# The last output projection: eight gated tiles multiplied by two weight blocks at a time in seven quarter products

## The chip, the cores and the metric

The kernel runs on one core of a Trainium2 chip. The metric is the device time of one execution, in microseconds (us). The time before is 1355.15 us, the median of three runs (1355.09 to 1355.34). TensorE (PE) multiplies matrices, VectorE (DVE), ScalarE (ACT) and GpSimd (POOL) work elementwise, and SyncE (SP) starts most transfers.

## The reference, cut to what matters

A two-layer trunk over 512 prompt tokens and 32 sample tokens. Layer 0 is an RWKV mixer, layer 1 a differential attention with twelve heads and a memory attention with four. Each layer ends in a gated branch of width 2048 and an output projection to width 1024:

```python
def diff_layer(...):
    ...
    o = rmsnorm(o, subln) * (1.0 - lam_init)
    y_mem = mem_attention(qm, mk, mv)
    out = jnp.concatenate([o.reshape(B, T, MIX_W).astype(x.dtype), y_mem], axis=-1) * jax.nn.silu(gate)
    return x + out @ w_out, k, v
...
y_prompt = rmsnorm(xp, final_norm_w)
y_sample = rmsnorm(xs, final_norm_w)
```

The change is about `out @ w_out` of layer 1, which is a 544x2048 by 2048x1024 product, and about what follows it, `x +` and the last `rmsnorm`.

## The kernel before, in words

Everything is kept transposed: features lie on the 128 partitions, tokens along the row. T = 544 tokens are cut in two halves of TH = 272. The gated branch is sixteen tiles `og0` to `og15` of 128x544 (`self.o1`). Tiles 0 to 7 are heads that are finished early; tiles 8 to 11 are the last four attention heads, and 12 to 15 the memory heads. The residual and the result is `x1` (128 x 8 x 544).

A product in fp32 is made from three matmuls. Each factor is split in a rounded high part and the rest: `hi = round(x)` is a copy on ACT, `lo = x - hi` is a subtraction on another engine, and hi·hi, lo·hi and hi·lo are accumulated in PSUM. A weight block is a column block of 128 outputs by 1024 inputs, loaded as two pieces of 256 KB (128x4x128); `split` makes `whi` and `wlo` from it, in two instructions each (128x512).

The output projection of layer 1 is `w_out`: eight output blocks k, sixteen tiles, two token halves and three matmuls, 768 matmuls of 128x272. It adds each finished block to `x1` in `consume`, which also squares it (ACT, `sqn`) and adds the squares up (DVE, `sums`). `consume` also issues the transposes of the finished `x1` to token rows (`ps_f`, on PE), the totals of the squares (`ps_n`, on PE), the last normalisation (`og<-ps_f`) and the stores of the result. After each finished pair of halves it starts one transfer of keys and values to the output (`kv_out`).

Ahead of it stands the main stream of layer 1 (`diff_layer`). A list of events `at(step, function)` puts attention work between the matmuls of the input projection, and while `self.ordered` is set every engine keeps the order of the program. The last head has seven blocks of 48 matmuls, 336 steps, counted from f. In it the split of gated tiles 4 to 7 is made at the steps `LATE` = 186, 222, 254 and 290. After the stream the remaining events run: the four heads of the last group are normalised (`norms`, the `oss` and `nt` operations), scaled (`ot<-ot,oss`), transposed by PE (`ps_oT`) and gated (`finished`, `og<-ps_oT`).

After the main stream the order is not the program's any more. A scheduler places the instructions by its own estimate of times, except on a queue that `self.tied` names, which is SP alone before. So the `ps_oT`, `ps_f` and `ps_n` work of PE lies where the scheduler finds place between the matmuls of `w_out`. A third pair of weight buffers (`self.third`, `w3`) serves every third block.

The helper through which nearly all instructions are recorded is one line, L132 before and L133 after, so operations are told apart by the names of their tiles.

Of the kernel before, what the change touches and what calls it, by code (L numbers as in the profile page):

```python
# [18 lines left out]
P = 128  # L19
# [46 lines left out]
NGATED = 8  # L66
EARLY = 4
# [67 lines left out]
class Trunk:  # L135
# [273 lines left out]
    def split(self, raw):  # L409
# [3 lines left out]
        third = self.third is not None and self.turn % 3 == 2  # L413
        self.turn += 1
        if third:
            both = self.third.tile([P, 2, KT, P], F32R, tag="hl", name="w3")
            hi, lo = both[:, 0], both[:, 1]
        else:
            hi, lo = (self.wp.tile([P, KT, P], F32R, tag=x, name=x, bufs=2) for x in ("whi", "wlo"))
# [910 lines left out]
    def gated(self, g, hi, lo, t):  # L1330

        self.ae.copy(hi[:], t)
        (self.nc.gpsimd if g % 2 and not self.third else self.ve).tensor_tensor(lo[:], t, hi[:].bitcast(F32), ALU.subtract)
# [14 lines left out]
    def w_out_blocks(self, i):  # L1348

        w = self.a["w_out"][i]  # L1350
        todo = [(0, 0), (1, 0), (0, 1), (1, 1)] + [(k, q) for k in range(2, KT) for q in range(2)]
        return [(w[q * D : (q + 1) * D, :], k * P) for k, q in todo]

    def w_out(self, i, p, order, consume, extra=None, o=None):
# [26 lines left out]
        if i:  # L1381
            units += units[-2:]
            parts[-2:] = [[halves[:1]]] * 2 + [[halves[1:]]] * 2

        def products():
            for n, ((k, q, gs, last), part) in enumerate(zip(units, parts)):
# [8 lines left out]
                for vs in part:  # L1395
                    for j, g in enumerate(gs):
                        if k < 2 and (j + k) % 2 == 0 and n >= first:
                            ahead(1)
                        if i and n == 1 and j == 2:
                            self.used()  # L1400
# [15 lines left out]
        return products(), ahead  # L1416

# [394 lines left out]
    def layer1(self):  # L1812
# [3 lines left out]
        self.o1 = [op.tile([P, T], F32, name=f"og{g}") for g in range(16)]  # L1816
        with ExitStack() as ectx:
            made, order = {}, list(range(8)) + [12, 13, 14, 15, 8, 9, 10, 11]
            with ExitStack() as c2:
# [5 lines left out]
                self.kz = [dq.tile([P, 2, T], F32R, name=f"kz{i}") for i in range(2)]  # L1825
# [4 lines left out]
                kv_out = self.diff_layer(dq, p, mp, mctx, lambda: self.pool("wo1e", 1, ctx=ectx, side="right"), order, made)  # L1830
# [3 lines left out]
            self.third, self.turn, self.tied = self.h0, 2, self.se  # L1834
# [32 lines left out]
            def consume(k, ps, v):  # L1867
# [3 lines left out]
                if k >= 2 and kv_out:  # L1871
                    kv_out.pop(0)()
# [12 lines left out]
            for _ in self.w_out(1, po, order, consume, o=made)[0]:  # L1885
                pass
        self.hctx.close()

    def stream(self, makes):

        def nxt():
            if self.made:
                return self.made.pop(0), []
            return self.split(self.early.pop(0))
# [22 lines left out]
        for fn, _ in cur[1]:  # L1917
            fn()
# [517 lines left out]
```

## Time and profile before

| what | value |
|---|---|
| median of three runs | 1355.15 us |
| the profiled execution | 1360.9 us |
| its span, first to last instruction | 1359.1 us |
| PE busy | 1304.9 us, 96% |
| DVE busy | 922.2 us, 68% |
| ACT busy | 856.3 us, 63% |
| POOL busy | 630.8 us, 46% |
| mean granted TensorE clock | 0.989 |

The profiled execution is 5.75 us longer than the median of the timed runs; 1.8 us of it lie outside its span. Positions below are us from the start of that span. The main stream of layer 1 ends at 1245.0, the matmuls of the output projection run from there to 1348.4, and the span ends at 1359.1. In a view of the timeline a row gives the start, the length, the engine, the line, the operation, its output and inputs, the shapes and the count; in square brackets stands how long the engine had waited and for what. Rows that follow each other closely on one engine overlap by a pipeline's depth, so the step from one to the next is a little shorter than the length.

### The profile page before, as it was taken

The numbers are of one execution on the slowest core, as the hardware profiler recorded it, in microseconds if no ns is written. First come the engines' busy times: TensorE is split into PE (matmuls) and PEld (weight loads), VectorE is DVE, ScalarE is ACT, GpSimd is POOL, SyncE is SP. The second block draws the span as 40 slices with busy tenths as digits, with TensorE's granted clock in tenths as the row PEclk, the third lists the DMA queues.
The fourth block names the chain that finished last, engine by engine and source line by source line (L and its number), as shares of the span: only waits on it lengthen the run. The fifth ranks groups of instructions, "written<-read, shape, count | busy, mean of one in ns | idle before, by whom it ended". The sixth has DMA issues, their size and how long they took to land. (4 is left out here: it accounts for less than half of the span.)

```text
span 1359.1 us, 32016 instructions
## 1 busy us (share of the span) xinstructions
PE 1304.9 (96%) x11713; PEld 1192.7 (88%) x11713; DVE 922.2 (68%) x2391; ACT 856.3 (63%) x2316; POOL 630.8 (46%) x1103
## 2 busy tenths in 40 slices
PE   6999999999999999989999999999999999999997
PEld 6998899999999999888889998888887887788997
DVE  6766667877787768766574453656697666877543
ACT  6665677677767777665554346777676776774421
POOL 1317675567556755660021007756555665662000
PEclk9999999999999999999999999999999999999999
DMA  7643223322332232232356444767677768774461
GB/s 235 183 118 78 61 69 87 78 73 73 87 78 70 76 87 74 55 104 73 114 186 202 130 133 130 172 160 177 148 185 164 174 156 183 172 172 115 143 203 66
DMA packets 418295, 171.52 MB, mean 126 GB/s; under 512 B 195209, under 2 KB 402578, under 8 KB 418138
## 3 DMA queue, kind: packets, MB, share of 16 engines
q1 hardware_dynamic: 417994, 168.96, 48.0%
q8 instruction: 92, 1.51, 0.5%
q14 instruction: 65, 0.53, 0.1%
q10 hardware_dynamic: 144, 0.52, 0.1%
HBM read 130.84 MB, written 41.92 MB: 127 GB/s over the span
## 5 line engine op out<-in xcount | busy, mean ns | idle before, releaser
L132 PE MATMUL ps_g<-h,whs 128*128 128x272 f16 x2688 | 334.1, 281 | 3.6 <-POOL whs L132 3.6
L132 PEld LDWEIGHTS <-whs 128*128 128x128 f16 x2688 | 256.9, 98 | 57.7 <-POOL whs L132 5.3
L132 PE MATMUL ps_g<-hl,whi 128*128 128x272 f32 x960 | 281.5, 298 | 0.6 <-POOL hl L591 0.5
L132 PE MATMUL ps_g<-hh,wlo 128*128 128x272 f32 x912 | 277.9, 305 | 1.3 <-DVE wlo L132 1.3
L132 PE MATMUL ps_g<-hh,whi 128*128 128x272 f32 x912 | 275.1, 302 | 0.9 <-ACT hh L132 0.9
L880 POOL TENSOR_TENSOR tm<-u,m 102x84 f32<-102x84 f32 (+23 forms) x372 | 157.3, 423 | 165.4 <-DMA m<-sc 134.8
L132 DVE TENSOR_TENSOR wlo<-raw,whi 128x512 fp32r<-128x512 f32 x194 | 140.8, 739 | 64.6 <-ACT whi L132 63.4
L132 PEld LDWEIGHTS ps_g<-hl,whi 128*128 128x128 f32 x960 | 181.6, 191 | 2.4 <-POOL hl L591 0.7
L132 PEld LDWEIGHTS ps_g<-hh,whi 128*128 128x128 f32 x912 | 174.8, 192 | 4.4 <-ACT hh L132 1.3
L132 PEld LDWEIGHTS ps_g<-hh,wlo 128*128 128x128 f32 x912 | 174.3, 191 | 4.8 <-DVE wlo L132 2.1
L882 POOL TENSOR_TENSOR u<-u,tm 102x84 f32<-102x84 f32 (+23 forms) x372 | 160.4, 431 | 29.1
L132 POOL TENSOR_TENSOR whs<-h16s,whs 128x512 f16<-128x512 f32 x112 | 130.7, 1187 | 51.4 <-ACT whs L132 49.7
L132 ACT CAST whi<-raw 128x512 fp32r<-128x512 f32 x194 | 116.2, 616 | 58.1 <-PE ps_g L132 31.0
L132 POOL TENSOR_SCALAR h16s<-h16s 128x512 f32<-128x512 f32 x112 | 79.1, 719 | 89.0 <-DVE h16s L132 83.0
L132 PE MATMUL ps_g<-hi,whi 128*128 128x272 f32 x384 | 110.7, 288 | 0.9 <-ACT whi L132 0.9
L132 PE MATMUL ps_g<-lo,whi 128*128 128x272 f32 x384 | 110.7, 288 | 0.7 <-DVE lo L132 0.7
L132 PE MATMUL ps_g<-hi,wlo 128*128 128x272 f32 x384 | 110.6, 288 | 0.2 <-DVE wlo L132 0.2
L132 DVE SCALAR_TENSOR_TENSOR SB<-ps_c,dl,sd 64x64 f32<-64x64 f32 x168 | 47.4, 282 | 43.5 <-PE ps_c L132 39.1
L132 PEld LDWEIGHTS ps_g<-hi,whi 128*128 128x128 f32 x384 | 72.2, 188 | 1.2 <-ACT whi L132 1.2
L132 PEld LDWEIGHTS ps_g<-lo,whi 128*128 128x128 f32 x384 | 72.2, 188 | 1.1 <-DVE lo L132 1.1
L132 PEld LDWEIGHTS ps_g<-hi,wlo 128*128 128x128 f32 x384 | 72.3, 188 | 0.4 <-DVE wlo L132 0.4
L132 ACT CAST whs<-h16s 128x512 f16<-128x512 f32 x112 | 65.4, 619 | 9.5 <-POOL h16s L132 7.7
(437 smaller groups left out, 2935.0 us busy)
## 6 DMA issues: line engine op xcount, KB each, us to landing
raw<-in_rw_in_dram SPq DMA_DIRECT2D x114, 256.0 KB
h16s<-in_df_in_dram SPq DMA_DIRECT2D x112, 256.0 KB
raw<-in_w_out_dram SPq DMA_DIRECT2D x56, 256.0 KB
ptr<-pk SPq DMA_DIRECT2D x44, 160.0 KB
aT<-ptr SPq DMA_DIRECT2D x11, 640.0 KB
scr<-sg SPq DMA_DIRECT2D x96, 68.0 KB
out_dram<-scr SPq DMA_DIRECT2D x6, 1024.0 KB
m<-sc SPq DMA_DIRECT2D x36, 128.0 KB
```

Of the source, the lines that this page charges most:

```text
L132: return lambda *a, **k: self.trunk.tie(self, issue(*a, **k))
L880: nc.gpsimd.tensor_tensor(tm[:, :n, :wd], u3[:, :n, kx : kx + 1].to_broadcast(sh), m3[:, kx : kx + 1, kx + 1 :].to_broadcast(sh), ALU.mult)
L882: nc.gpsimd.tensor_tensor(u3[:, :n, kx + 1 :], u3[:, :n, kx + 1 :], tm[:, :n, :wd], ALU.add)
```

## The change

The product of tiles 0 to 7 with the eight output blocks is made by Strassen's method in Winograd's form. For a pair of output blocks (n = 0 to 3) the weight is cut in four quarters (input half by output block), the tiles in four (four tiles by token half, 128 x 4 x 272). Seven products of a quarter sum with a quarter sum replace eight. Each is a group of 4 x 3 = 12 matmuls; 28 groups make 336 matmuls where 384 were. Tiles 8 to 15 are multiplied as before (384 matmuls).

Around that:

- **Weights.** For each pair four sums of weight pieces on DVE (`sum`, 128x512), seven copies on ACT, six subtractions on POOL and one on DVE (`ws`). Group t prepares group t + 3. The sums lie in the same four raw buffers (`h16s`) through which the pieces are loaded; the order of the pieces is now all first input halves, then all second ones.
- **Tokens.** Seven quarter sets in high and low parts, each in two instructions of 128x544: sets 1, 2 and 3 are raw quarters (steps 40 and 100 of heads 10 and 11, 186 and 222 of the last), with the low part on POOL; sets 7, 6, 4 and 5 are differences (`d7`, `d6`, `d4`, `d5` on DVE), made and split at the steps 258 to 343 of the last head.
- **Results.** Each product is added to, or subtracted from, `x1` by DVE (`add`, 128x272), eight times for a pair.
- **Order.** After the stream PE is tied to the program's order as SP is (`self.tied` is now a pair). The remaining events run between the matmuls of the groups, and `finished` moves from b + 30 to b + 48. The `kv_out` transfers start one for every 24 matmuls.
- **Removed.** The third weight buffer; the subtraction for odd gated tiles is on POOL again.

```diff
-        if self.ordered or self.tied is queue:
+        if self.ordered or self.tied and queue in self.tied:
...
-        third = self.third is not None and self.turn % 3 == 2
...
-        (self.nc.gpsimd if g % 2 and not self.third else self.ve).tensor_tensor(lo[:], t, hi[:].bitcast(F32), ALU.subtract)
+        (self.nc.gpsimd if g % 2 else self.ve).tensor_tensor(lo[:], t, hi[:].bitcast(F32), ALU.subtract)
...
+        if i:
+            todo = [(k, q) for q in range(2) for k in range(KT)]
...
+    def parted(self, to, x, q, low):
+        hi, lo = to[0][q], to[1][q]
+        self.ae.copy(hi, x)
+        low.tensor_tensor(lo, x, hi.bitcast(F32), ALU.subtract)
+    def seven(self, blocks, sets, groups, add, free):
...
+        def prepare(t):
...
+            if i == 7:
+                sum_of(n, 3, a11, a21)
+            if i == 6:
+                sum_of(n, 1, a21, a22)
+                sum_of(n, 2, sums[n, 1], a11)
+            if i == 4:
+                sum_of(n, 4, sums[n, 2], a12)
...
+            self.ae.copy(hi, x)
+            def low():
+                (self.ve if i == 5 else self.ge).tensor_tensor(lo, x, hi.bitcast(F32), ALU.subtract)
...
+        def products():
...
+                for k in range(4):
+                    for j, (w, x) in enumerate(((hi, xh), (hi, xl), (lo, xh))):
+                        if k == 0 and j == 0:
+                            low = prepare(t + 3)
+                        if k == 1 and j == 1:
+                            low()
...
+    def w_out1(self, blocks, load, sets, tiles, add, consume):
+        groups = [(2, 0), (1, 0), (2, 1), (7, 0), (6, 0), (1, 1), (4, 0), (5, 0), (7, 1), (3, 0), (6, 1), (4, 1), (2, 2), (5, 1)]
+        groups += [(1, 2), (7, 2), (3, 1), (6, 2), (4, 2), (2, 3), (5, 2), (1, 3), (7, 3), (3, 2), (6, 3), (4, 3), (5, 3), (3, 3)]
...
+            for n, (k, vs) in enumerate([(k, halves) for k in range(KT - 2)] + [(k, [v]) for v in halves for k in (KT - 2, KT - 1)]):
...
+            def add(k, v, ps, up):
+                x = self.x1[:, k, v]
+                self.ve.tensor_tensor(x, x, ps, ALU.add if up else ALU.subtract)
...
-            self.third, self.turn, self.tied = self.h0, 2, self.se
...
-                        at(b + 30 + 14 * j, lambda G=G, hg=hg, j=j: finished(G, hg, j))
+                        at(b + 48 + 14 * j, lambda G=G, hg=hg, j=j: finished(G, hg, j))
...
+                plan = [(186, lambda: raw_set(3, 0)), (222, lambda: raw_set(3, 1)), (258, lambda: fresh(7))]
+                plan += [(258 + 8 * q, lambda q=q: differ(7, q, B[0, 1][q], B[1, 1][q])) for q in range(2)]
+                plan += [(286, lambda: (fresh(6), fresh(4)))]
+                plan += [(286 + 4 * q, lambda q=q: differ(6, q, tmp[7][q], B[0, 0][q])) for q in range(2)]
+                plan += [(294 + 4 * q, lambda q=q: differ(4, q, tmp[6][q], B[1, 0][q], ALU.add)) for q in range(2)]
+                plan += [(300 + 6 * q, lambda q=q: split(7, q)) for q in range(2)]
+                plan += [(312 + 6 * q, lambda q=q: split(6, q)) for q in range(2)]
+                plan += [(290 + 16 * t, lambda t=t: begun(t)) for t in range(3)]
+                plan += [(337, late)] + [(337 + q, lambda q=q: split(4, q)) for q in range(2)]
+                plan += [(338, lambda: fresh(5))] + [(339 + q, lambda q=q: differ(5, q, B[0, 0][q], B[0, 1][q])) for q in range(2)]
+                plan += [(341 + q, lambda q=q: split(5, q)) for q in range(2)]
...
-        self.used()
-        self.ordered = False
+        self.ordered, self.tied = False, (self.te, self.se)
         while ev:
-            ev.pop(0)[2]()
+            i += 1
+            while ev and ev[0][0] <= i:
+                ev.pop(0)[2]()
+            next(begun(None))
```

Three places show how instructions stand now. The first is DVE in the last head, from one attention output to the weights of the next scores (`ot` is the output of the third of the last four heads, `pt` the scores' weights for PE's transposes). Before:

```order
L132 TENSOR_SCALAR h16s<-dv,h16s 128x1
L132 TENSOR_TENSOR ot<-ps_o,os_16820 128x512
L132 TENSOR_TENSOR kz_12354<-og_12335,kz_12354 128x544
L132 TENSOR_REDUCE oss<-ps_o 128x4
L132 SCALAR_TENSOR_TENSOR og_12339<-og_12339,ps_g 128x272
L132 COPY os<-ps_os 128x128
L132 RECIPROCAL srs<-srs 128x1
```

The same place of the changed kernel:

```order
L133 TENSOR_SCALAR h16s<-dv,h16s 128x1
L133 TENSOR_TENSOR sum<-h16s 128x512 x2
L133 TENSOR_TENSOR sum<-sum,h16s 128x512 x2
L133 TENSOR_TENSOR sum<-h16s 128x512
L133 TENSOR_TENSOR ot<-ps_o,os_16805 128x512
L133 TENSOR_TENSOR d_18262<-og 128x544
L133 TENSOR_REDUCE oss<-ps_o 128x4
L133 SCALAR_TENSOR_TENSOR og<-og,ps_g 128x272
L133 COPY os<-ps_os 128x128
L133 TENSOR_TENSOR d_18262<-og 128x544
L133 RECIPROCAL srs<-srs 128x1
```

Five weight sums stand ahead of `ot`, the last of them of weight pieces that are loaded late, and the two halves of `d7` stand where the split of tile 6 (`kz`) was.

The second place is DVE after the stream, from the last head's square totals (`oss`) to its scaled output (`ot<-ot,oss`), for which PE's transposes `ps_oT` wait. Before, the middle of it:

```order
L132 SCALAR_TENSOR_TENSOR oss<-nt_18473,oss 128x16
L132 TENSOR_TENSOR w_18582<-h16s,w_18582 128x512
L132 TENSOR_TENSOR nt_18473<-oss 128x16
L132 TENSOR_TENSOR w_18582<-h16s,w_18582 128x512
L132 TENSOR_TENSOR nt_18473<-nt_18473,oss 128x16
L132 SCALAR_TENSOR_TENSOR nt_18473<-nt_18473 128x16
L132 SCALAR_TENSOR_TENSOR oss<-nt_18473,oss 128x16
L132 TENSOR_TENSOR ot<-ot,oss 128x512 x3
```

The same of the changed kernel:

```order
L133 TENSOR_TENSOR x_10643<-x_10643,ps_g 128x272
L133 SCALAR_TENSOR_TENSOR oss<-nt_18473,oss 128x16
L133 TENSOR_TENSOR late<-d_18484,late 128x544
L133 TENSOR_TENSOR nt_18473<-oss 128x16
L133 TENSOR_TENSOR x_10643<-x_10643,ps_d 128x272
L133 TENSOR_TENSOR nt_18473<-nt_18473,oss 128x16
L133 SCALAR_TENSOR_TENSOR og<-osT,h16s,og 128x32
L133 SCALAR_TENSOR_TENSOR nt_18473<-nt_18473 128x16
L133 SCALAR_TENSOR_TENSOR og<-osT,h16s,og 128x32
L133 SCALAR_TENSOR_TENSOR oss<-nt_18473,oss 128x16
L133 TENSOR_TENSOR sum<-sum,h16s 128x512
L133 TENSOR_TENSOR ot<-ot,oss 128x512 x4
```

The chain is now interleaved with the additions to `x1` (which wait for PE), with two low parts (`late`) and with a weight sum. PE's first `ps_oT` stands, in its fixed order, behind 50 matmuls of the groups.

The third place is the end of PE's order, at the second to last block of the first token half and the one behind it. Before:

```order
L132 MATMUL ps_g<-lo_17527,w_19340 128x272
L132 MATMUL ps_f<-ident,x_10643 128x128 x2
L132 MATMUL ps_g<-hi_17526,w_19340 128x272
L132 MATMUL ps_g<-hi_17727,w_19340 128x272
L132 MATMUL ps_g<-lo_17728,w_19340 128x272
L132 MATMUL ps_g<-hi_17727,w_19340 128x272
L132 MATMUL ps_g<-hi_17872,w_19340 128x272
L132 MATMUL ps_n<-ones,sums 128x1 x2
L132 MATMUL ps_g<-lo_17873,w_19340 128x272
```

The same of the changed kernel:

```order
L133 MATMUL ps_g<-lo_18690,whi 128x272
L133 MATMUL ps_g<-hi_18689,wlo 128x272
L133 MATMUL ps_n<-ones,sums 128x1 x2
L133 MATMUL ps_f<-ident,x_10643 128x128 x2
L133 MATMUL ps_g<-hi_18675,whi 128x272
L133 MATMUL ps_g<-lo_18676,whi 128x272
```

The totals `ps_n` stood ten matmuls behind the block whose squares they add up, and stand now directly behind its last matmul; the other transposes `ps_f` are placed in the same way.

More of the change, by code (lines that the diff above doesn't have):

```diff
@@ L66 @@
 NGATED = 8
+RAW_SETS = {1: (0, 0), 2: (1, 0), 3: (1, 1)}
 EARLY = 4
@@ L412, in split @@
             return self.split_scaled(raw)
-        third = self.third is not None and self.turn % 3 == 2
[L414 to L419, printed above, removed]
+        hi, lo = (self.wp.tile([P, KT, P], F32R, tag=x, name=x, bufs=2) for x in ("whi", "wlo"))
         todo = []
@@ L1815, in layer1, with load, begun @@
         op = self.pool("o1", 1)
-        self.o1 = [op.tile([P, T], F32, name=f"og{g}") for g in range(16)]
+        self.og = op.tile([P, 16, T], F32, name="og")
+        self.o1 = [self.og[:, g] for g in range(16)]
         with ExitStack() as ectx:
-            made, order = {}, list(range(8)) + [12, 13, 14, 15, 8, 9, 10, 11]
+            sets, tiles, steps, blocks = {}, {}, [], []
+            def load():
+                if self.ahead:
+                    for _ in self.load_steps(*self.ahead.pop(0)):
+                        pass
+                    blocks.append(self.early[-1])
+            def begun(t):
+                if not steps:
+                    blocks.extend(self.early)
+                    while len(blocks) < 4:
+                        load()
+                    steps.extend(self.w_out1(blocks, load, sets, tiles, add, lambda *x: steps[2](*x)))
+                return steps[1] if t is None else steps[0](t)()
+            def add(k, v, ps, up):
+                x = self.x1[:, k, v]
+                self.ve.tensor_tensor(x, x, ps, ALU.add if up else ALU.subtract)
             with ExitStack() as c2:
@@ L1883, in consume, with gate @@
                     last((2, 3, 4) if v.start else (0, 1))
-            for _ in self.w_out(1, po, order, consume, o=made)[0]:
-                pass
+            steps.append(consume)
+            left = [12, 13, 14, 15, 8, 9, 10, 11]
+            tiles.update((g, self.fetch(po, g)) for g in left)
+            def gate(g):
+                tiles[g] = self.gated(g, *tiles[g])
+            for n, _ in enumerate(steps[1]):
+                if n % 24 == 23:
+                    if left:
+                        gate(left.pop(0))
+                    if kv_out:
+                        kv_out.pop(0)()
         self.hctx.close()
@@ L2396, in run @@
         self.early, self.made, self.ahead = [], [], []
-        self.third, self.turn, self.inner, self.rec, self.tied = None, 0, False, None, None
+        self.inner, self.rec, self.tied = False, None, None
         self.mctx = ExitStack()
```

136 lines of the change are left out of this document (110 added, 26 removed).

## The prediction

> **What bounds the kernel now.** First the busy shares and the granted clock on the page, then the windows of the output projection, then the chain of work that ended last.
>
> ```profile
> PE 1304.9 (96%) x11713; PEld 1192.7 (88%) x11713; DVE 922.2 (68%) x2391; ACT 856.3 (63%) x2316; POOL 630.8 (46%) x1103
> ...
> 1225.00:1235.00 10.00, 10.00 (x93) 8.15 (x91) 5.77 (x17) 5.17 (x14) 4.44 (x5) 1.00 0.78 214
> 1235.00:1245.00 10.00, 9.92 (x88) 8.66 (x86) 7.73 (x22) 4.87 (x12) 3.81 (x3) 1.00 0.26 73
> 1245.00:1252.00 7.00, 6.67 (x55) 6.48 (x53) 6.38 (x22) 3.22 (x7) 0.00 (x0) 1.00 0.00 0
> 1260.00:1300.00 40.00, 40.00 (x323) 39.85 (x323) 20.38 (x38) 13.09 (x27) 0.00 (x0) 1.00 0.55 173
> 1300.00:1340.00 40.00, 40.00 (x323) 39.87 (x322) 12.64 (x24) 8.10 (x16) 0.00 (x0) 1.00 0.38 122
> ...
> 1300.31 30.62 PE ps_g L132 x245
> ```
>
> In a row of the windows stand the stretch, its length, and busy us (and count) of PE, PE's weight loads, DVE, ACT and POOL, then the granted clock, 1.00 here. PE never rests from 1225 on but for 0.4 us, and POOL does nothing at all in the projection. In the chain 245 matmuls in a row take 30.62 us, 0.125 us each. So a matmul less is 0.125 us less, as long as PE stays as busy; and a wait of PE, which is nearly nothing now, is a loss in full:
>
> ```profile
> PE ps_n L132 <- DVE sums L132: 0.5, 1, 0.5
> PE ps_oT L132 <- DVE ot L132: 0.3, 1, 0.3
> PE ps_f L132 <- DVE x L132: 0.2, 1, 0.2
> ```
>
> These are all of PE's waits from 1225 to the end (us, times, longest).
>
> **What the change removes.** 384 matmuls become 336: 48 x 0.125 = **6.0 us less** on PE. The weight loads are as many as the matmuls and fit beside them now (39.85 of 40 us). This is certain; the rest is what new waits take back. I go through PE's fixed order at three places.
>
> **The last head.** DVE's rows, with those of SP and PE, from the timeline and the chain of before (the short rows are the chain's):
>
> ```profile
> 1229.74 0.69 DVE L132 TENSOR_TENSOR ot<-ps_o,os 128x512 f32<-128x512 f32 x1 [1.62 <-PE ps_o L132]
> ...
> 1238.09 0.44 DVE L132 SCALAR_TENSOR_TENSOR og<-og,ps_g 128x272 f32<-128x272 f32 x1 [1.68 <-ACT og L132]
> ...
> 1239.07 0.75 DVE L132 SCALAR_TENSOR_TENSOR pt<-ps_s,srs,pt 128x512 f32<-128x512 f32 x1
> ...
> 1228.31 2.63 SPq L132 DMA_DIRECT2D h16s<-in_w_out_dram  x2
> ...
> 1202.08 2.01 DMA scr<-sg
> ...
> 1230.53 0.60 ACT ps_o L132
> 1231.13 0.30 ACT pk L132
> ...
> 1231.71 0.43 PE L132 MATMUL ps_os<-cv,aTs 128*32 128x128 f32 x8
> ...
> 1239.97 0.63 PE L132 MATMUL ps_aT<-ident,pt 128*128 128x128 f32 x4
> ```
>
> Five weight sums now stand ahead of `ot`. The idle 1.62 us before it hold two and a half of them (0.64 each, from `wlo`, 1.28 for two, below). The fifth needs the seventh weight piece, which SP issues at 1228.31, when POOL has freed its buffer; I take 2.0 us for the transfer, the length of `scr<-sg`, the nearest one in the chain of waits. The piece is there near 1230.4, and `ot` follows at 1231.1 instead of 1229.74, 1.4 us late. PE's `ps_os` waits behind `ot` and two short ACT steps of the chain, which ended at 1231.43, so 0.3 us of that are covered: 1.1 us of PE at least. With the sums held up by POOL (next paragraph) I find up to 3.7. Ahead of `pt` stand three more pieces of 128x544, the second half of `d6` and both of `d4`, behind an `og` that now ends the idle time: 3 x 0.66 = 2.0 us, less the 0.15 between `pt`'s end (1239.82) and `ps_aT`. So 1.8 us without contention, and up to 5 with. The start of the projection moves by **3 to 9 us; I take 5**, nearer the rows without contention, since POOL's idle times leave room.
>
> **The engines' contention.** What two engines do to each other is in these rows:
>
> ```profile
> 1238.67 1.34 POOL L1333 TENSOR_TENSOR vhl<-og,khl 128x544 fp32r<-128x544 f32 x1 [8.12 <-ACT khl L132]
> 1239.98 2.50 POOL L132 TENSOR_TENSOR wlo<-h16s,whi 128x512 fp32r<-128x512 f32 x2
> ...
> 1240.17 1.10 DVE L132 SCALAR_TENSOR_TENSOR nt<-os 128x1 f32<-128x1 f32 x1
> 1241.30 1.19 DVE L132 TENSOR_TENSOR nt<-nt,os 128x1 f32<-128x1 f32 x1
> 1242.53 0.16 DVE L132 SCALAR_TENSOR_TENSOR os<-nt,os 128x1 f32<-128x1 f32 x1
> ```
>
> One DVE operation on a single column takes 1.10 us while POOL's first `wlo` runs, the next 1.19 while the second runs, and 0.16 as soon as POOL is done: DVE stood still for the whole of POOL's operation. The projection is free of this before, with POOL at 0.00; the change puts 26 POOL subtractions there (22 `ws`, four `lo` of odd tiles).
>
> [...]
>
> **The groups.** DVE's list between the last `ot` and the scaled `ot`, for which `ps_oT` waits:
>
> ```profile
> 1246.47 1.28 DVE L132 TENSOR_TENSOR wlo<-h16s,whi 128x512 fp32r<-128x512 f32 x2
> ...
> 1248.74 0.68 DVE L132 TENSOR_TENSOR w<-h16s,w 128x512 fp32r<-128x512 f32 x1
> 1249.34 0.17 DVE L132 TENSOR_TENSOR nt<-oss 128x16 f32<-128x16 f32 x1
> 1249.43 0.68 DVE L132 TENSOR_TENSOR w<-h16s,w 128x512 fp32r<-128x512 f32 x1
> ...
> 1250.65 1.90 DVE L132 TENSOR_TENSOR ot<-ot,oss 128x512 f32<-128x512 f32 x3
> ...
> 1251.48 0.63 PE L132 MATMUL ps_oT<-ident,ot 128*128 128x128 f32 x4 [0.33 <-DVE ot L132]
> ...
> L132 DVE TENSOR_TENSOR x<-ps_g,x 128x272 f32<-128x272 f32 x16 | 6.9, 442 | 25.0 <-PE ps_g L132 25.0
> ...
> L132 DVE TENSOR_TENSOR lo<-og,hi 128x544 fp32r<-128x544 f32 x8 | 5.3, 719 | 0.0
> L132 ACT CAST whi<-raw 128x512 fp32r<-128x512 f32 x16 | 9.1, 619 | 22.3 <-PE ps_g L132 17.3 <-issue 4.2 <-ACT sums L132 0.8
> ```
>
> Four low parts go (2.5 us by their steps). In come two `d5` and two `late` at 0.66 (5.3 us for eight, in the groups by line), three additions to `x1` at 0.44 and a sum at 0.64: 4.6 us, of which 0.6 fit in an idle piece ahead of `oss`. `ot` is ready 1.5 us later against PE, which comes 2 to 3 matmuls (0.3 us) later, and already waited 0.33. PE is tied, so nothing moves up into the gap: **1.5 us**. POOL has there two `late` of 1.34 (by `vhl`) and three `ws` of 1.25 (by its `wlo`), 6.4 us, against DVE operations that read two tiles; if DVE stands still for all of it the wait is 7.9 us. Behind that, POOL has 21 operations of about 1.25 us (26 us) and DVE some 20 two-operand ones holding about 0.5 us (10 us), 36 us in 35 us of matmuls for the remaining groups: 0 to 4 us more. **1.5 to 12 us; I take 5**, as POOL must run in that stretch but DVE's additions read PSUM and need not stop.
>
> The eight additions for a pair (32 x 0.44 = 14 us) and the casts of ACT (28 x 0.62 = 17 us, by `whi<-raw`, 619 ns) stand beside 42 us of matmuls, on engines that were busy for half of the time and a third: nothing. If that cover were gone each group would wait 0.44 for its addition, 12 us; groups on the same bank are two or more groups apart, so I leave it at nothing. The `kv_out` transfers go on SP, now between weight pieces; the DMA share there is 0.55 at most, also nothing.
>
> **The end.** PE is tied behind each wait for `x1` or for `sums`:
>
> ```profile
> 1295.59 0.87 PE ps_f L132 x8
> ...
> 1296.07 0.69 DVE L132 TENSOR_TENSOR og<-ps_f,fw 128x512 f32<-128x512 f32 x1
> ...
> 1296.81 0.66 PE L132 MATMUL ps_f<-ident,x 128*128 128x128 f32 x4
> ...
> 1330.97 0.44 DVE L132 TENSOR_TENSOR x<-ps_g,x 128x272 f32<-128x272 f32 x1 [1.20 <-PE ps_g L132]
> 1331.97 0.44 DVE L132 TENSOR_TENSOR sums<-sums,sqn 128x272 f32<-128x272 f32 x1 [0.56 <-ACT sqn L132]
> ```
>
> From a block's last matmul to the end of `x` are 0.55 us, to the end of `sums` (1332.41) 1.45. Twenty `ps_f` in a row wait 0.55, then have two banks, which DVE empties in 0.7 us each with one `sums` between, for five: 4.0 us in all where the transposes alone need 2.2 (eight in 0.87 in the chain, which is the first row): 1.8. Six, then six again: 0.55 each. `ps_n`: 1.45. Sum 4.35, less the 0.2 that is there now: **4.1 us** (2.5 if the banks don't bind and a neighbouring wait covers one of them, 5 at most). The last `ps_n`, behind the last block, is the same in both kernels.
>
> **The sum.** Against the profiled execution's 1360.9 us (span 1359.1): -6.0 + 5 + 5 + 4.1 = +8.1. The timed median is 5.75 us lower for the same program, and I carry the difference over: 1355.15 + 8.1 = **1363 us**.
>
> **The rivals.**
> - *As above*, three waits of moderate size: 1363, from 1358 to 1370. Chance 0.45.
> - *The lock decides.* Every POOL operation stops a two-operand one of DVE, so the upper ends hold: -6 + 9 + 12 + 4.1 = +19, **1374 us**. For it speaks the doubled `nt` above; against it, that many DVE operations read PSUM. [...] Chance 0.2.
> - *Only the end stays.* DVE's additions in the last head fit in its idle times and `ps_oT` is not late, because POOL is ahead: -6 + 4.1 = -1.9, **1353 us**, within 0.2%. Against it speaks the fifth sum's load, for which DVE stands still. Chance 0.15.
> - *The saving arrives: faster.* One mechanism, in the last head: the weight pieces land before 1229, since their buffers come free earlier, so that all sums fit in DVE's 1.62 idle us and everything on DVE and POOL stays ahead of PE to the end of the groups. Then the end at its lower price is what is left: -6 + 2.5 = -3.5, **1351.6 us**. It decides at the seventh piece: 1.5 us earlier or not. Chance 0.2.
>
> That the matmuls are not fewer can be left out: the order of PE shows 336.
>
> **The range.** 0.2% (2.7 us) is about what a measurement of this kernel tells from no change. Faster by more: the last case, 0.2. Within: the third, 0.15. Slower: 0.65. From 1350.5, which takes in the faster case but for its edge, to 1376, with the lock's case: about 0.8 with what lies beyond either. The forecast's own range is 1358 to 1370.
>
> **What would show it.** Right: in the waits of PE from 1225 on, `ps_os` or `ps_aT` behind DVE's `ot` or `pt` with 1 us or more each; `ps_oT` behind `ot` with 1.5 or more; `ps_n` behind `sums` with two waits near 1.4; `ps_f` behind `x` and `og`. The stage's POOL busy goes from 0 to about 30 us, and DVE's `sum` and `late` are longer than 0.7 in the mean. Wrong: the projection's start still at 1245; PE at 40 of 40 in each window; or two-operand operations of DVE at 0.66 beside POOL.

## The result and the profile after

The changed kernel takes 1377.47 us, the median of six runs (1374.28 to 1382.05); the kernel before took 1355.14 us beside it (six runs, 1353.15 to 1355.8). The ratio, here and below taken over the single runs and not from the two medians, is 1.0169, with a 95% interval from 1.0149 to 1.019: slower, by about 22 us. The sign is the forecast's. The size is not: 1363 was forecast, and the time lies 7.5 us beyond the forecast's own range (1358 to 1370) and 1.5 us beyond the wide one (up to 1376), nearest to the rival in which the lock decides (1374).

The profiled execution took 1382.05 us (span 1380.3). Its busy line and all of PE's waits from 1200 us on (total us, times, longest):

```profile
PE 1310.2 (95%) x11665; PEld 1194.4 (87%) x11665; DVE 957.6 (69%) x2433; ACT 870.0 (63%) x2334; POOL 679.8 (49%) x1135
...
PE ps_g L133 <- DVE x L133: 5.2, 2, 2.9
PE ps_aT L133 <- DVE pt L133: 4.2, 2, 3.3
PE ps_g L133 <- DVE oss L133: 3.8, 1, 3.8
PE ps_n L133 <- DVE sums L133: 3.2, 2, 1.6
PE ps_os L133 <- ACT pk L133: 3.1, 1, 3.1
PE ps_oT L133 <- DVE ot L133: 2.4, 1, 2.4
PE ps_f L133 <- DVE og L133: 0.6, 2, 0.3
PE ps_f L133 <- DVE x L133: 0.6, 2, 0.3
```

There are 48 matmuls fewer (11713 before), and yet PE is busy for 5.3 us longer. Before, the waits from 1200 on came to 2.3 us: the 1.0 from 1225 on that the prediction shows, and one of 1.3 at `ps_aT` ahead of it. Now they are 23.1 us, but waits are no busy time: something else makes the matmuls themselves longer. The windows around the waits show what (columns as in the prediction: PE, weight loads, DVE, ACT, POOL, then the granted clock, and last the DMA engines' busy share and GB/s):

```profile
1229.00:1232.00 3.00, 2.72 (x23) 1.44 (x24) 2.42 (x7) 1.11 (x4) 0.00 (x0) 0.50 0.00 0
1232.00:1235.00 3.00, 3.00 (x11) 1.97 (x10) 1.42 (x5) 0.08 (x1) 0.00 (x0) 0.50 0.00 0
1235.00:1238.00 3.00, 3.00 (x26) 2.48 (x25) 1.49 (x4) 2.64 (x7) 0.00 (x0) 0.92 0.00 0
...
1242.00:1245.00 3.00, 1.37 (x7) 1.19 (x8) 2.93 (x6) 0.25 (x1) 3.00 (x3) 0.55 0.09 28
1245.00:1249.00 4.00, 4.00 (x20) 3.47 (x19) 2.62 (x13) 0.88 (x2) 1.47 (x1) 0.50 0.61 180
...
1264.00:1269.00 5.00, 4.82 (x23) 4.83 (x23) 3.98 (x8) 0.62 (x1) 0.65 (x1) 0.50 0.17 52
...
1282.00:1286.00 4.00, 1.20 (x9) 1.23 (x10) 4.00 (x5) 1.19 (x3) 4.00 (x4) 1.00 1.03 362
...
1294.00:1298.00 4.00, 4.00 (x24) 4.00 (x23) 3.39 (x6) 0.62 (x1) 2.52 (x3) 0.63 0.59 184
...
1360.00:1365.00 5.00, 4.98 (x29) 4.99 (x30) 2.87 (x11) 1.34 (x2) 0.00 (x0) 0.68 0.17 60
```

After most waits of PE of 2.4 us and more the granted clock is 0.50 (not after the one of 2.85 us, in the window from 1282 to 1286), and a matmul of 128x272 takes 0.226 us from one to the next instead of 0.125. Busy time by the missing share of the clock, summed over these rows (2.72 x 0.50 + 3.00 x 0.50 + 3.00 x 0.08 + ... ), is about 11.2 us: as an estimate, that is what the slow clock cost, and no wait shows it.

The stretch from the third attention output of the last head (PE's `ps_o`) to the span's end, cut by positions of PE's matmuls in the timelines of the profiled executions, in us:

| stage | before | after | more | waits of PE in it, after |
|---|---|---|---|---|
| A: rest of the last head | 17.7 | 29.6 | 11.9 | 6.4 |
| B: the 28 groups | | 60.3 | | 11.4 |
| C: the matmuls behind them | | 58.0 | | 2.8 |
| B and C | 103.4 | 118.3 | 14.9 | 14.2 |
| D: last normalisation | 10.7 | 10.7 | 0 | 1.6 |
| all | 131.8 | 158.6 | 26.8 | |

Three things in the experiments need this table. First, the medians differ by 22.3 us and the profiled executions by 21.2 (1360.9 before), but these stretches by 26.8: the third `ps_o` lies at 1227.3 before and at 1221.8 after, and between 1217.7 and 1227.3 in all profiles of this study. What lies ahead explains it: in the profile before PE waited there for 41.9 us, and its busy time by the missing share of the clock comes to 11.9 us; in the one after they are 38.1 and 9.8, together 5.9 us less. In every profile of the study the third `ps_o`, less these two sums, lies between 1171.4 and 1174.3. Up to 1172 us the engines have the same instructions in the same order in both kernels, and 5.2 of the 5.5 us stand at 1024 already. So a time moves by some us with what lies ahead, and the stage is the sharper reading. Second, without waits and at the full clock B would take about 44.0: 103.4 before, less its 0.3 of waits, the 6.0 of the 48 matmuls and 53.1 for C (measured in the experiment on the end). Third, what is above the wait-free length and is not a wait (5.5 in A, 4.9 in B, 2.1 in C: 12.5) is the clock, of which the windows above account for 11.2.

Where the waits come from is read off the rows of DVE, POOL and PE in the last head, from the timeline of the changed kernel:

```profile
1222.47 2.25 DVE L133 TENSOR_TENSOR sum<-h16s 128x512 f32<-128x512 f32 x2
1224.76 2.25 DVE L133 TENSOR_TENSOR sum<-sum,h16s 128x512 f32<-128x512 f32 x2
1226.94 0.69 DVE L133 TENSOR_TENSOR sum<-h16s 128x512 f32<-128x512 f32 x1
1227.55 0.68 DVE L133 TENSOR_TENSOR ot<-ps_o,os 128x512 f32<-128x512 f32 x1
...
1222.66 3.08 POOL L133 TENSOR_TENSOR whs<-h16s,whs 128x512 f16<-128x512 f32 x2
...
1229.28 0.66 PE L133 MATMUL ps_os<-cv,aTs 128*32 128x128 f32 x8 [3.07 <-ACT pk L133]
...
1238.11 4.21 DVE L133 TENSOR_TENSOR d<-d,og 128x544 f32<-128x544 f32 x3
...
1239.92 1.82 POOL L133 TENSOR_TENSOR khl<-d,h 128x544 fp32r<-128x544 f32 x1
...
1243.63 1.09 PE L133 MATMUL ps_aT<-ident,pt 128*128 128x128 f32 x4 [3.32 <-DVE pt L133]
```

Four sums ahead of `ot` take 4.5 us, most of it beside POOL's `whs`; the fifth, when POOL is done, takes 0.69, without any wait for its load. The output `ps_o` is complete at 1224.1, and `ot` starts 3.4 us later: as an estimate 1.4 of it are five sums at the step of 0.61 us that the fifth, 0.69 long, shows, from 1222.47 on, and 2.0 are `whs`. Three pieces of `d6` and `d4` take 4.21 us beside POOL's subtractions, where 3 x 0.66 were expected. In the groups the same happens to an addition to `x1`, which frees a PSUM bank for PE:

```profile
1281.10 1.51 DVE L133 TENSOR_TENSOR ws<-sum,ws 128x512 fp32r<-128x512 f32 x1
1282.53 1.78 DVE L133 TENSOR_TENSOR lo<-og,hi 128x544 fp32r<-128x544 f32 x1
1284.23 0.42 DVE L133 TENSOR_TENSOR x<-x,ps_g 128x272 f32<-128x272 f32 x1
...
1284.80 1.36 PE L133 MATMUL ps_g<-late,ws 128*128 128x272 f32 x9 [2.85 <-DVE x L133]
```

The addition itself takes 0.42 us, as before. It is late because the two operations ahead of it in DVE's order take 3.3 us instead of 1.4. In the window from 1282 to 1286 above, DVE and POOL are both busy for 4.00 of 4.00 us, PE for 1.20.

### The profile page after: what moved, and what is told of

Its sections match the earlier page's. It is cut to its first block, busy times and chain, and to the rows that moved or that the text cites. A ratio compares the mean times of both kernels' runs of the same rounds, so it can differ in the third digit from the quotient of the medians.

```text
span 1380.3 us, 32061 instructions
## 1 busy us (share of the span) xinstructions
PE 1310.2 (95%) x11665; PEld 1194.4 (87%) x11665; DVE 957.6 (69%) x2433; ACT 870.0 (63%) x2334; POOL 679.8 (49%) x1135
## 3 DMA queue, kind: packets, MB, share of 16 engines
q8 instruction: 92, 1.51, 0.4%
## 5 line engine op out<-in xcount | busy, mean ns | idle before, releaser
L133 PE MATMUL ps_g<-hl,whi 128*128 128x272 f32 x912 | 271.0, 297 | 0.5 <-POOL hl L586 0.5
L133 PEld LDWEIGHTS ps_g<-hl,whi 128*128 128x128 f32 x912 | 173.5, 190 | 2.4 <-POOL hl L586 0.7
L133 DVE TENSOR_TENSOR wlo<-raw,whi 128x512 fp32r<-128x512 f32 x178 | 128.9, 734 | 47.5 <-ACT whi L133 46.6
L133 ACT CAST whi<-raw 128x512 fp32r<-128x512 f32 x178 | 107.3, 618 | 36.3 <-issue 19.3
L133 ACT CAST whs<-h16s 128x512 f16<-128x512 f32 x112 | 65.6, 620 | 11.4 <-POOL h16s L133 8.9
```

Of the source, the lines that this page charges most:

```text
L133: return lambda *a, **k: self.trunk.tie(self, issue(*a, **k))
```

## The experiments

### Is it POOL's reading that stops DVE?

Copies on ACT in place of POOL's subtractions of the weights, which this kernel leaves out (`e2_low_act`):

```diff
-                (self.ve if i == 5 else self.ge).tensor_tensor(lo, x, hi.bitcast(F32), ALU.subtract)
+                if i == 5:
+                    self.ve.tensor_tensor(lo, x, hi.bitcast(F32), ALU.subtract)
+                else:
+                    self.ae.copy(lo, x)
```

> The changed kernel, with the 24 low parts of the weights that POOL makes replaced by a copy on ACT (the subtraction is left out, so the product's small terms are wrong). Theory (DVE's two-operand operations stand still while POOL works): DVE's sum and lo operations in the groups go from 1.4 to 1.9 us down to about 0.7, PE's waits of 2.4 to 3.8 us in the groups fall from 11.4 us in all to under 4, and the time falls by 9 to 14 us, to about 1366. Rival (the order of DVE's queue alone makes the waits): these operations stay long or the waits stay, and the time falls by 3 us at most.

Measured: 1365.07 us (1364.66 to 1365.77), ratio to before 1.0071 (1.0056 to 1.0086): 12.4 us of the loss are gone. B falls from 60.3 to 49.4 us and its waits from 11.4 to 3.5. A, in which the weights of the first three groups are made, is 4.7 us shorter as well (24.9), and C, where the slow clock is gone, 1.6. So the weights' subtractions on POOL cost about half of the loss. But is that because POOL reads, or because POOL is in the chain of the weights? In the next kernel (`e6_low_set`) POOL stays in the chain and nearly as busy (23.0 us from 1262 to 1300, 26.7 in the changed kernel), but for the weights it only writes:

```diff
-                (self.ve if i == 5 else self.ge).tensor_tensor(lo, x, hi.bitcast(F32), ALU.subtract)
+                if i == 5:
+                    self.ve.tensor_tensor(lo, x, hi.bitcast(F32), ALU.subtract)
+                else:
+                    for _ in range(2):
+                        self.ge.memset(lo.bitcast(F32), 0.0)
```

> The changed kernel, with each of the 24 low parts that POOL makes replaced by two memsets of the same tile on POOL (about 0.7 us each by the 0.21 us of a 128x128 one, so POOL is busy as long as before but reads nothing; the subtraction is left out). Theory (what stops DVE is POOL reading or working on SBUF beside a two-operand operation): if reading is what matters, DVE's operations are at 0.7 us, PE's waits in the groups fall as in e2_low_act (3.5 us in all) and the time is 1365 to 1368. If POOL's writing alone stops DVE, they stay near 1.4 us and the time near 1377. Rival (e2_low_act was faster because ACT makes a low part in 0.62 us where POOL takes 1.3 or more): the waits in the groups stay above 8 us, 1374 or more, with DVE's operations short.

Measured: 1367.33 us (1363.24 to 1370.62), ratio 1.0085 (1.0052 to 1.0117), B 51.6 us with 5.0 of waits. The costliest groups between 1262 and 1300 (total us, mean ns of one), of the changed kernel:

```profile
L133 DVE TENSOR_TENSOR lo<-og,hi 128x544 fp32r<-128x544 f32 x4 | 7.0, 1752 | 0.0
L133 DVE TENSOR_TENSOR sum<-sum,h16s 128x512 f32<-128x512 f32 x6 | 6.4, 1064 | 0.0
L133 DVE TENSOR_TENSOR sum<-h16s 128x512 f32<-128x512 f32 x4 | 5.1, 1267 | 0.0
...
L133 POOL TENSOR_TENSOR ws<-sum,ws 128x512 fp32r<-128x512 f32 x7 | 10.5, 1507 | 10.4 <-ACT ws L133 10.4
```

The same stretch of the kernel whose POOL fills with zeros:

```profile
L133 DVE TENSOR_TENSOR lo<-og,hi 128x544 fp32r<-128x544 f32 x4 | 5.8, 1450 | 0.2 <-ACT hi L133 0.2
L133 DVE TENSOR_TENSOR sum<-sum,h16s 128x512 f32<-128x512 f32 x5 | 3.4, 684 | 0.0
L133 DVE TENSOR_TENSOR sum<-h16s 128x512 f32<-128x512 f32 x4 | 2.7, 682 | 0.0
...
L133 POOL MEMSET ws<- 128x512 f32 x34 | 17.7, 527 | 15.0 <-PE ps_g L133 12.0 <-PE ps_d L133 1.6 <-ACT ws L133 0.5
L1328 POOL TENSOR_TENSOR lo<-og,hi 128x544 fp32r<-128x544 f32 x4 | 5.5, 1376 | 0.7 <-ACT hi L133 0.7
```

POOL is busy for 23 of 38 us here, and the sums take 0.68 us beside the fills, as in the kernel before a `w` of the same shape at 1248.74 with POOL idle. DVE's `lo`, beside POOL's own reading `lo` (1.38 us), still takes 1.45 instead of 0.72, and `ws` 0.87 in the mean instead of 0.69. So what stretches DVE's sums in these rows is POOL's subtractions, which read SBUF (1.06 and 1.27 us), not that POOL is busy or late: the fills, which only write, leave them at 0.68. The loss is also mutual: in the changed kernel POOL's `ws` takes 1.51 us in the mean of the rows above, and 1.29 at 1252.25 in the same trace, where DVE has no two-operand subtraction or sum.

### Is the order of DVE's queue enough?

The next kernel (`e1_sums_behind`) takes the weight sums out of the last head, behind everything that DVE has to do there:

```diff
-            self.ve.tensor_tensor(t, x, y, ALU.add)
+            ins = self.ve.tensor_tensor(t, x, y, ALU.add)
+            if not self.ordered:
+                self.order(ins, self.ve.last)
```

> The changed kernel with one edit: no weight sum may stand ahead of the last DVE instruction of the main stream. Theory (sums in DVE's queue, slowed by POOL, and TensorE's clock that falls to 0.50 after a long wait): PE's wait of 3.07 us at ps_os goes, and with it the stretch at clock 0.50 behind it, 5 to 7 us less than 1377.5, so about 1371; one or two us of it may come back as longer waits in the groups. Rival (the sums only fill time in which DVE would wait anyway, and ps_os is late for another reason): the wait at ps_os stays at 2 us or more and the time within 2 us of 1377.

Measured: 1380.9 us (1379.05 to 1385.23), ratio 1.0198 (1.0178 to 1.0219): no gain, where 1371 was expected. The wait of `ps_os` is gone and A is 6.5 us shorter (23.1), but B is 7.4 us longer (67.7). So the reading of the place was right (the sums made `ot` late) and the expected gain was not kept: B has 14.4 us of waits instead of 11.4, and more of the slow clock. That it is the same sums beside the same POOL subtractions is the likely cause; this kernel alone does not show it.

### The end

PE is released from the program's order behind the groups (`e3_free_end`):

```diff
+                if n == 28 * 12:
+                    self.tied = (self.se,)
```

> The changed kernel, with PE free of the program's order from the end of the seven products on, so that the transposes and totals of the end are placed between matmuls as before. Theory: the waits behind x, og and sums (0.35 + 0.29 + 0.32 + 1.53 + 0.32 us) and the stretch at clock 0.50 near 1362 go, 3.5 to 5.5 us less than 1377.5, so about 1373. Rival (the waits only change place): within 1.5 us of 1377.

Measured: 1375.64 us (1373.14 to 1377.39), ratio 1.0147 (1.0132 to 1.0163). PE's waits at `ps_n` fall from 3.2 us to 0.5, and those at `ps_f` from 1.2 to 0.2, as in the kernel before.

C goes from 58.0 to 53.1 us, 4.9 less, and the clock stays at 1.00 there. The median is only 1.8 us lower, within the spread of both kernels. That the tie of PE costs 4.9 us in its stage is shown; that it costs as much in the median is not.

### What does a wait of PE cost?

This was the most important question, and it can be asked of the kernel before, whose projection has no waits. Into its stream of matmuls goes a chain on DVE between two sets of four transposes, so that PE waits once for about 4.3 us (`e4_stall`):

```diff
-            for _ in self.w_out(1, po, order, consume, o=made)[0]:
-                pass
+            for n, _ in enumerate(self.w_out(1, po, order, consume, o=made)[0]):
+                if n == 480:
+                    self.tied = self.te
+                if n == 492:
...
+                    self.ve.tensor_copy(scr[0][:], ps[:])
+                    for i in range(5):
+                        self.ve.tensor_tensor(scr[1 - i % 2][:], scr[i % 2][:], scr[i % 2][:], ALU.mult)
...
+                if n == 504:
+                    self.tied = self.se
```

> The kernel before, with one wait of PE put into the output projection, where PE is never idle: four transposes, a copy and five products of 128x512 on DVE behind them, and four transposes that wait for the last. By the rows of before DVE needs about 0.3 + 5 x 0.62 = 3.4 us, so PE waits some 3.5 us. If a wait of this length halves TensorE's clock for several us: 5.5 to 7.5 us more than 1355.1. If a wait costs only its own length: 4.0 to 4.7 us more (the wait and eight transposes), and the granted clock stays at 1.00 throughout.

The other kernel (`e5_stall_full`) has the same chain, and 30 transposes more in the place where PE waited:

```diff
+                    fl = self.psm.tile([P, 512], F32, tag="m", name="ps_fl")
+                    for i in range(30):
+                        self.te.transpose(fl[:, i % 4 * P : i % 4 * P + P], self.ident[:], self.ident[:])
```

> The kernel of e4_stall with thirty more transposes of 128x128 on PE inside the wait (30 x 0.11 = 3.3 us, the wait was 4.31), so that PE works where it waited. Theory (an idle PE loses its clock): the granted clock stays at 1.00 behind the wait, and the kernel is 1 to 2 us faster than e4_stall's 1362.3, though it does more. Rival (the clock fell there for another reason): the clock falls as in e4_stall and the time is the same or up to 1 us longer.

Windows of the kernel with the wait:

```profile
1306.00:1310.00 4.00, 0.70 (x7) 0.46 (x5) 3.86 (x7) 0.00 (x0) 0.00 (x0) 1.00 0.83 277
1310.00:1314.00 4.00, 2.99 (x16) 3.02 (x17) 0.83 (x2) 0.00 (x0) 0.00 (x0) 0.70 0.49 169
1314.00:1318.00 4.00, 4.00 (x30) 4.00 (x29) 0.00 (x0) 0.53 (x1) 0.00 (x0) 0.87 0.00 0
```

Windows of the kernel in which the wait is filled:

```profile
1310.00:1314.00 4.00, 2.97 (x27) 2.76 (x26) 2.47 (x4) 0.00 (x0) 0.00 (x0) 1.00 0.88 300
1314.00:1318.00 4.00, 4.00 (x34) 4.00 (x34) 0.00 (x0) 0.35 (x1) 0.00 (x0) 1.00 0.07 23
```

In the first the clock falls to 0.70 and 0.87 in the mean of four us, and 16 and 30 matmuls are done where the filled one does 27 and 34 (transposes included). In the second it never leaves 1.00. In position, B and C together grow from 103.4 to 110.5 us with the wait (7.1: 4.3 of waiting, 0.9 of eight transposes, and about 1.7 of clock, which is 4.00 x 0.30 + 4.00 x 0.13 by the rows, as PE is busy for the whole time at 0.50, from 1311.6 to 1315.0) and to 108.9 with it filled: 30 transposes more, and 1.6 us less. The medians do not show it: 1362.25 us (1359.29 to 1363.81), ratio 1.0047 (1.0032 to 1.0063), and 1362.4 (1359.28 to 1365.2), ratio 1.0049 (1.0032 to 1.0065). So the traces show that this wait of 4.3 us takes the clock along (0.70 and 0.87) and that work in its place keeps it (1.00); the difference of 1.6 us in the stage is too small for these runs' times to confirm, and the expected gain in time is not there.

The kernel before had shown the same in the prediction's own profile, ahead of the stage that was read. A row of its timeline, and its windows:

```profile
831.78 0.64 PE L132 MATMUL ps_g<-h,whs 128*128 128x272 f16 x3 [2.86 <-POOL whs L132]
...
829.00:832.00 3.00, 0.21 (x2) 0.20 (x3) 0.07 (x1) 1.02 (x3) 2.95 (x5) 1.00 0.01 3
832.00:835.00 3.00, 3.00 (x16) 2.17 (x15) 0.00 (x0) 0.00 (x0) 2.89 (x5) 0.51 0.59 172
835.00:838.00 3.00, 3.00 (x26) 2.45 (x25) 0.00 (x0) 0.86 (x2) 3.00 (x4) 0.92 0.41 112
```

One wait of 2.86 us, and 16 matmuls in the next three us where the three us after them have 26. The table of the time before said as much in one number: a mean granted clock of 0.989 leaves 1.1% of 1359.1 us, about 15 us, that were not granted, although every window of the projection shows 1.00.

### What is left when the order is mended?

Five kernels ask whether a better order of the same work would let the saving through. The first (`e7_moved`) has the sums behind the last head, PE free at the end, and the differences at quieter steps; the splits of the remaining gated tiles start only after step 60 of the groups:

```diff
-                plan += [(258 + 8 * q, lambda q=q: differ(7, q, B[0, 1][q], B[1, 1][q])) for q in range(2)]
+                plan += [(252 + 2 * q, lambda q=q: differ(7, q, B[0, 1][q], B[1, 1][q])) for q in range(2)]
...
-                plan += [(286 + 4 * q, lambda q=q: differ(6, q, tmp[7][q], B[0, 0][q])) for q in range(2)]
-                plan += [(294 + 4 * q, lambda q=q: differ(4, q, tmp[6][q], B[1, 0][q], ALU.add)) for q in range(2)]
+                plan += [(266 + 2 * q, lambda q=q: differ(6, q, tmp[7][q], B[0, 0][q])) for q in range(2)]
+                plan += [(282 + 2 * q, lambda q=q: differ(4, q, tmp[6][q], B[1, 0][q], ALU.add)) for q in range(2)]
...
-                    if left:
+                    if left and n > 60:
```

> The changed kernel complete, with four things moved: the weight sums behind the main stream (as e1), d7, d6 and d4 into DVE's idle times of the last head (steps 252, 266 and 282), the gated tiles' splits later among the groups, PE free at the end (as e3). Theory: the last head gives back most of its 12 us and the end 5; the groups keep their port conflict, so 12 to 18 us remain there: 1362 to 1368. Rival (each wait that goes comes back in full in the groups, as in e1): 1374 or more.

Measured: 1374.35 us (1371.4 to 1376.16), ratio 1.0135 (1.0101 to 1.0168). A is nearly mended (19.0, waits 0.8), C is (53.1), and B is the longest of all kernels: 68.0, with 16.1 of waits. The time is the rival's (1374 or more) and not the theory's (1362 to 1368). Its three largest waits:

```profile
PE ps_d L133 <- DVE x L133: 5.3, 2, 4.9
PE ps_g L133 <- DVE x L133: 4.1, 2, 2.9
PE ps_oT L133 <- DVE ot L133: 3.6, 1, 3.6
```

Then the heads' work goes five groups further back, to ask whether one urgent chain is at fault (`e10_late_heads`; the gated tiles' splits again from the start of the groups, PE untied at step 180 already):

```diff
-                        at(b + 48 + 14 * j, lambda G=G, hg=hg, j=j: finished(G, hg, j))
+                        at(b + 108 + 14 * j, lambda G=G, hg=hg, j=j: finished(G, hg, j))
```

> As e7_moved, with the four last heads' transposes and gating 60 matmuls later (step b + 108 instead of b + 48) and the gated tiles' splits at their first places again. It tells whether the waits in the groups are those of one urgent chain in DVE's queue or of the whole amount of two-operand work. Theory (amount: POOL's and DVE's operations exclude each other for more time than the groups last): the wait at ps_oT goes, others grow, and the stretch from osT to the first remaining matmul stays above 60 us (68.0 in e7_moved, 43.8 without waits); 1370 to 1375. Rival (one urgent chain): the stretch falls under 55 us and the time to 1362 or less.

Measured: 1372.96 us (1370.43 to 1373.68), ratio 1.0119 (1.0082 to 1.0155). The wait of `ps_oT` (3.6) is gone, yet B is still 64.9 us with 13.2 of waits, now on `x`, 4.9 and 3.7 us; the second lies at 1286.6, behind step 180, where PE is not tied any more. That speaks for the amount of work by which POOL and DVE slow each other, and against one chain. The next kernel (`e11_late_split`) shares it differently, with six of the low parts on DVE instead of POOL:

```diff
-                (self.ve if i == 5 else self.ge).tensor_tensor(lo, x, hi.bitcast(F32), ALU.subtract)
+                (self.ve if i == 5 or n and i in (6, 7) else self.ge).tensor_tensor(lo, x, hi.bitcast(F32), ALU.subtract)
```

> As e10_late_heads, with six of POOL's 24 low parts of weights moved to DVE (products 6 and 7 of the last three pairs). Each takes about 0.6 us of DVE alone where it took 1.3 of POOL and stopped DVE as long. Theory (amount of excluded work): 6 x 0.6 us less of it, so 2 to 5 us less than e10_late_heads. Rival (DVE's own length is the bound): 2 to 4 us more.

Measured: 1369.53 us (1367.55 to 1371.06), ratio 1.0096 (1.006 to 1.0132); B 62.6, waits 10.6. An operation of 1.3 us on POOL (`ws`, 1.29 at 1252.25 of the changed kernel), beside which DVE's sums take 1.06 and 1.27 us in the mean, is 0.7 us on DVE itself (0.69 at 1266.85), and the gain of 2.3 us in B is what six such exchanges leave. It is no repair.

Last, both orders with ACT copies in place of POOL's subtractions (the edit of the first experiment): the moved kernel (`e9_moved_act`), and the one with the late heads (`e12_late_act`).

> As e7_moved, with the low parts of the weights by ACT copies instead of POOL's subtractions (the subtraction is left out, as in e2). Theory (lock, queue order and fixed end are all there is): what remains is the saving of 6 us, less 1 to 5 us of waits for DVE: 1350 to 1356, at or below the kernel before. Rival (seven products cost something in themselves, through the additions to x1 or the weight loads of twelve-matmul groups): 1360 or more.

> As e10_late_heads, with POOL's low parts replaced by ACT copies (the subtraction is left out, as in e2). What the seven products would give if neither the lock nor the urgent chain nor the fixed end were there. Theory: the stretch of the groups at 44 to 48 us, 1350 to 1354. Rival (the groups have a cost of their own): above 50 us and 1357 or more, as e9_moved_act's 51.8 and 1358.5.

Measured: 1358.54 us (1354.69 to 1360.79, ten runs), ratio 1.0021 (1.0008 to 1.0035), and 1359.39 us (1353.81 to 1361.25, ten runs), ratio 1.001 (0.9988 to 1.0031). B is 51.8 and 51.4, with 5.4 and 4.1 of waits. Even so neither is faster than before, and both miss what the theory gave them (1350 to 1356, and 1350 to 1354); the second lies where its rival had it. The largest wait that is left is one of 3.2 us in both. Rows of DVE, POOL and PE from the timeline of the late heads' kernel:

```profile
1248.97 1.31 DVE L133 TENSOR_SCALAR oss<-oss 128x16 f32<-128x16 f32 x1
1250.83 1.33 DVE L133 TENSOR_SCALAR oss<-oss 128x16 int32<-128x16 int32 x1
...
1248.50 3.63 POOL L133 TENSOR_TENSOR late<-d,late 128x544 fp32r<-128x544 f32 x2 [5.56 <-DVE og L133]
...
1255.30 3.15 PE L133 MATMUL ps_g<-hl,ws 128*128 128x272 f32 x12 [3.17 <-ACT ws L133]
```

Two operations on 16 columns take 1.3 us each beside POOL's two `late`, and the second ends where POOL does (1252.16 and 1252.13); the weight sum behind them is late, so ACT's `ws` is, and so PE is. The twelve matmuls that follow take 3.15 us, at half the clock. From the third `ps_o` to the span's end this kernel takes 133.6 us, where 131.8 less the saving of 6.0 would be 125.8; the wait (3.2) and the clock behind it (2.7) are 5.9 of these 7.8 us. No kernel of this study is faster than the kernel before.

## Why the prediction was right in sign and wrong in size

In the profiled executions, by stage (us). "Clock" is what the stage has beyond the wait-free length and the waits:

| term | forecast (range) | measured | of it waits | of it clock |
|---|---|---|---|---|
| 48 matmuls less | -6.0 | about -6 | | |
| the last head | 5 (3 to 9) | 11.9 | 6.4 | 5.5 |
| the groups | 5 (1.5 to 12) | 16.3 | 11.4 | 4.9 |
| the end | 4.1 (2.5 to 5) | 4.9 | 2.8 | 2.1 |
| sum | +8.1 | +27.1 | 20.6 | 12.5 |

The sum is 0.3 above the 26.8 of the stages, which still hold the 0.3 us of waits before.

- **The saving arrived.** In the kernel with late heads and ACT copies, B less its waits (4.1) and the clock behind them (2.7) is 44.6, and C 53.1: 97.7 us together where 103.1 were without waits, 5.4 less.
- **"A wait of PE ... is a loss in full" is the step that failed.** The prediction priced each wait at its own length. Most of these waits cost their length and then the clock: 12.5 us of the 27.1 are no waits, and the windows' clock accounts for about 11.2 of them. No term, bound or rival held this, and rows that show it (831.78) stood in the trace that was read. With the clock left out the measured waits would have given -6 + 20.6 = 14.6, a time near 1370, at the upper end of the forecast's own range.
- **The contention was seen and priced too low.** `nt` at 1.10 and 1.19 us was the right row, and the lock's case, in which POOL's operations stop DVE's, came nearest. The forecast took values near the undisturbed rows because POOL's idle times would leave room; the runs show 6.4 us of waits in the last head (5 taken, bounds 3 to 9) and 11.4 in the groups (5 taken, bounds 1.5 to 12), so the groups are the term that was mis-sized in waits, near its upper bound. POOL is busy for 40.4 us in the groups, where about 30 were forecast; its own operations are stopped too (`ws` 1.43 and 1.51 us in the mean there, 1.25 forecast). With POOL only writing, B's waits fall to 5.0, without the subtractions to 3.5, so most of the groups' waits come with POOL's subtractions. For the groups' 0 to 4 us more, DVE's operations were taken to hold POOL for about 0.5 us each: an estimate that no run shows. What the runs show is POOL's `ws` at 1.29 us where DVE has no sum or subtraction, and at 1.43 and 1.51 in the groups' mean. Nor does a run show a port or a lock, which the prediction and the expectations name; measured are the lengths on both engines: DVE's sums at 1.06 and 1.27 us beside POOL's subtractions, and 0.68 beside its fills.
- **The last head, in detail.** The five sums and the three pieces did stand in the way, as said. But the fifth sum did not wait for its load (it follows the fourth without a pause); of the 3.4 us by which `ot` was late, about 2.0 came from POOL's `whs`, which was there before the change too.
- **Additions to `x1` were costed at nothing**, since they lie beside matmuls on a half idle DVE. The additions read PSUM and are not slowed themselves (0.43 us), as the prediction said. But they queue behind operations that are, and 9.0 of the 11.4 us of waits in the groups are put down to them (`x`, 5.2) or to the operation behind one (`oss`, 3.8: an addition that frees a bank ends at 1261.18, and PE goes on at 1261.33). The cover was the idle half of DVE, and the stretched operations had used it up.
- **The end: the mechanism was right, its number in part luck.** Freeing PE takes 4.9 us from the stage, where 4.1 were forecast. But only 2.8 of them are waits, and the clock, which was not priced, made up for the rest. The `ps_n` behind the second to last block waits 1.53 us (1.45 forecast); the other wait of `ps_n` (1.62) is the last one, which D holds. The waits at `ps_f` come to 1.2 us, where 2.9 (1.8 + 0.55 + 0.55) were worked out.

What stays open: why the waits ahead of the stage, in code that is the same, differ from one execution to the next. They are why the profiled executions differ by 21.2 us and their stages by 26.8; that the medians differ by 22.3 for the same reason is likely, but they have no profile. And no run frees PE from the program's order in the first 15 groups, so what the tie itself costs there is not shown.

## What to carry to other kernels

When one engine holds the bound without pauses, price a new wait of it at its length and at what follows it (here 3.4 or 6.8 us at a clock of 0.50 behind most waits of 2.4 us and more), and look in the trace of before for the nearest wait of that size and the clock behind it (here 2.86 us at 831.78, then 0.51). When a change puts POOL operations that read SBUF beside DVE ones that read two tiles there (here sums of 0.68 us took 1.06 and 1.27 in the mean, and POOL's `ws` 1.51 instead of 1.29), add their times up, as an upper estimate, as if both ran on one engine, and ask whether that sum fits in the stage; if it does not, another order only moves the wait. Fewer matmuls are a gain only where the sums and splits that replace them find room on engines which can run at the same time.

## What the runs showed of the hardware

**Behind waits shorter than 3 us the clock fell to 0.50, and not always.** In the changed kernel, read in windows of 0.2 us, the clock falls to 0.50 near 1228.7, 1242.3 and 1262.8 and rises again near 1235.5, 1249.1 and 1269.6, each time after about 6.8 us. After the falls near 1293.5 and 1361.8 it rises after 3.4 us, as it does in the kernel with the single wait (1311.6 to 1315.0) and in the kernel before (832.06 to 835.47). Placed within its window by the window's mean clock, each of the ten falls and rises lies within 0.01 us of a multiple of 3.413 us from the first: the last rise, 1365.20, lies 136.53 us, or 40 of these steps, behind the first fall, 1228.67. So the clock changes here only at steps of 3.41 us, and these rows differ in how a wait lies to them:

```profile
1279.87:1283.28 3.41, 2.08 (x17) 1.86 (x15) 3.41 (x4) 3.32 (x6) 3.41 (x3) 1.00 0.99 350
1283.28:1286.70 3.42, 1.90 (x15) 1.93 (x16) 3.42 (x5) 0.12 (x1) 3.42 (x3) 1.00 1.06 361
1290.11:1293.52 3.41, 1.01 (x9) 0.82 (x7) 3.41 (x6) 0.77 (x2) 3.41 (x3) 1.00 0.40 106
1293.52:1296.94 3.42, 3.42 (x15) 3.42 (x16) 3.39 (x5) 0.36 (x1) 2.29 (x2) 0.50 0.43 128
```

The wait of 2.85 us is cut by a step's end at 1283.28: PE is idle for 1.33 us of one step and 1.52 of the next, and the clock stays. The wait of 2.40 us lies whole in one step, and the next step is at 0.50. The other falls follow steps in which PE was idle for 2.46, 2.01, 2.93 and, near the end, 1.54 us; a step with 1.81 idle us (from 1255.98) has none behind it, so no sharp bound comes out of these rows. In this trace each rise comes behind a step in which PE was busy throughout (3.41 of 3.41 us from 1232.12, 1266.22 and 1361.79, 3.42 of 3.42 from 1245.76 and 1293.52); the three steps at 0.50 that begin with 0.6 to 1.4 us of the wait still in them (from 1228.71, 1242.35 and 1262.81) are followed by a second one at 0.50. What sets these steps no run shows.

**A short one-input operation of DVE was stretched as well**: 1.31 and 1.33 us for `oss` on 16 columns beside POOL's `late`. In the kernel before the same two take 0.17 each, with no POOL operation beside them.
